# Row-wise infinity norm of an 8192 x 8192 matrix: smaller loads, more buffers, two load queues, and a tail in shrinking pieces

## The chip, the cores and the metric

The kernel runs on one core of a Trainium2 chip. The metric is the device time of one execution in microseconds (us), as a median over executions. A profile measures a span that is 1.7 to 2.1 us shorter than the time of the same execution. Its one-page summary is called the page here. Every run that is quoted here was fast, with the full clock granted (1.0 in the records).

Some words for what follows. In the traces each load appears as packets on 16 DMA engines: one packet for each partition's contiguous run of bytes, so 128 packets for a load of 128 partitions, eight on each engine (4,096 for the 32 loads of the kernel before). After its packets each engine makes a 4-byte semaphore write, the signal that VectorE waits for (528 writes in that trace, 16 for each of its 33 transfers). A load has landed when all 16 writes are in. A queue holds what one engine has issued. The exposed end is the reduce work that is left after the last landing.

## The reference

```python
def reference(x):                     # x: 8192 x 8192 float32, normally distributed
    return np.linalg.norm(x, ord=np.inf, axis=1)
```

For each row this is the largest absolute value in the row. The input is 268.4 MB and the output 32 KiB, so the work is to read the input once.

## The kernel before

The 8192 rows lie on 128 partitions, 64 rows on each. One load brings two neighbouring rows to every partition: 64 KiB per partition, 8 MiB in all. One VectorE reduce follows per load. There are three such buffers, and all loads go out from the SyncE queue.

```python
    x_t = x.rearrange("(a p n b) c -> a n p (b c)", p=P, a=A, n=N, b=B)   # A=8, N=4, B=2
    sbuf = ctx.enter_context(tc.tile_pool(name="sbuf", bufs=BUFS))        # BUFS=3
    r_all = outp.tile([P, A, N, B], mybir.dt.float32)

    for a in range(A):
        for n in range(N):
            t = sbuf.tile([P, bc], x.dtype)                               # bc = 16384
            t_b = t.rearrange("p (b c) -> p b c", b=B, c=cols)
            # ... a branch that is never taken is cut ...
            nc.sync.dma_start(out=t[:], in_=x_t[a, n])
            nc.vector.reduce_max(
                out=r_all[:, a, n, :], in_=t_b[:],
                axis=mybir.AxisListType.X, apply_absolute_value=True,
            )

    nc.sync.dma_start(out=out_t[:], in_=r_all[:])
```

Of the kernel before, what the change touches and what calls it, by code (L numbers as in the profile page):

```python
# [1 line left out]
logging.getLogger("concourse").setLevel(logging.ERROR)  # L3

# [1 line left out]

# [4 lines left out]


@with_exitstack
def kernel(
    ctx: ExitStack,
    tc: tile.TileContext,
    x: bass.AP,
    out: bass.AP,
    A: int = 8,
    B: int = 2,  # L20
    K: int = 4,
    BUFS: int = 3,
):
    nc = tc.nc
    P = nc.NUM_PARTITIONS

    rows, cols = x.shape
    assert rows % P == 0
    n_tiles = rows // P

    assert n_tiles % (A * B) == 0
    N = n_tiles // (A * B)
    x_t = x.rearrange("(a p n b) c -> a n p (b c)", p=P, a=A, n=N, b=B)
    out_t = out.rearrange("(a p n b) -> p a n b", p=P, a=A, n=N, b=B)

    bc = cols * B
    c_k = bc // K

    sbuf = ctx.enter_context(tc.tile_pool(name="sbuf", bufs=BUFS))
    outp = ctx.enter_context(tc.tile_pool(name="outp", bufs=1))  # L40

    r_part = outp.tile([P, N, K], mybir.dt.float32)
    r_all = outp.tile([P, A, N, B], mybir.dt.float32)

    for a in range(A):
        split = False
        for n in range(N):
            t = sbuf.tile([P, bc], x.dtype)
            t_b = t.rearrange("p (b c) -> p b c", b=B, c=cols)
            src = x_t[a, n]  # L50
            if split:
                for k in range(K):
                    nc.sync.dma_start(
                        out=t[:, k * c_k : (k + 1) * c_k],
                        in_=src[:, k * c_k : (k + 1) * c_k],
                    )
                    nc.vector.reduce_max(
                        out=r_part[:, n, k : k + 1],
                        in_=t[:, k * c_k : (k + 1) * c_k],
                        axis=mybir.AxisListType.X,  # L60
                        apply_absolute_value=True,
                    )
                nc.vector.reduce_max(
                    out=r_all[:, a, n, :],
                    in_=t_b[:],
                    axis=mybir.AxisListType.X,
                    apply_absolute_value=True,
                )
            else:
                nc.sync.dma_start(out=t[:], in_=src)  # L70
                nc.vector.reduce_max(  # L71
                    out=r_all[:, a, n, :],
                    in_=t_b[:],
                    axis=mybir.AxisListType.X,
                    apply_absolute_value=True,
                )

    nc.sync.dma_start(out=out_t[:], in_=r_all[:])


# [1 line left out]
_INS = ['x']  # L82
_OUTS = [((8192,), 'float32')]


# [23 lines left out]
```

## Time and profile before

| what | before | where it is read |
|---|---|---|
| time | 644.97 us | timed runs |
| span of the profiled run | 643.6 us | page |
| VectorE busy | 551.0 us | page, engines |
| first load packet starts | 1.76 us | packet records |
| last load packet ends / last load landed | 622.92 / 623.36 us | packet and semaphore records |
| reduce after that landing | 17.24 us | timeline |
| end of the last reduce to the end of the span | 2.98 us | timeline, page |

The page cuts the span into 40 slices. A digit is the busy share of a slice in tenths, and the last line is what the DMA engines moved in each slice, in GB/s:

```profile
DVE  0588898888998888998888988888988888988888
DMA  9999999999999999999999999999999999999960
GB/s 391 456 399 448 444 403 456 391 456 444 403 456 444 403 456 440 407 456 436 411 456 432 415 456 424 424 456 407 440 456 399 448 452 399 452 444 403 456 261 2
```

The DMA engines are at 9 until the end, while VectorE (DVE) is at 8 in most slices. The GB/s swing between slices because a packet of 64 KiB is booked where it lies: a slice is 16.1 us, in which six packets on each engine make 391 GB/s and seven make 456. The packets themselves are steadier. There are 4,096 packets of 65,536 bytes with a median of 2,420 ns, and their durations sum to 621.2 us per DMA engine, the same as the distance from the first packet's start to the last one's end. Followed along one engine, nearly every packet starts 3 to 4 ns before the record of the one before it ends. An engine is hardly ever without a packet. The loads are the bound.

The group of the reduces (line, engine, operation, names, shapes, count; busy us, mean ns of one; idle time before them and what ended it), and the profile's end in order of time (start us, duration, engine, line, operation, and in brackets the idle time before it):

```profile
L71 DVE TENSOR_REDUCE r_all<-t 128x2 f32<-128x16384 f32 x32 | 551.0, 17220 | 89.6 <-DMA t<-in_x_dram 89.6
```

```profile
604.03 17.22 DVE L71 TENSOR_REDUCE r_all<-t 128x2 f32<-128x16384 f32 x1 [2.12 <-DMA t<-in_x_dram]
623.38 17.22 DVE L71 TENSOR_REDUCE r_all<-t 128x2 f32<-128x16384 f32 x1 [2.13 <-DMA t<-in_x_dram]
640.62 0.40 SPq L78 DMA_DIRECT2D out_dram<-r_all  x1
```

VectorE waits 2.1 us for every load, so it is off the critical path everywhere except after the last landing. There a whole reduce of 17.22 us runs with nothing beside it, and then the output is stored. This 17.22 us is what the change can shorten. It should not lengthen the 621 us of loads.

### The profile page before, as it was taken

The page shows a single profiled execution, that of the slowest core. Times are in us where ns is not written, and L with a number is a line of the kernel's source. Part 1 is how long each engine was busy: PE and PEld are TensorE (multiplying, and loading weights), DVE is VectorE, ACT ScalarE, POOL GpSimd, SP SyncE. Part 2 cuts the span into 40 slices and gives each one's busy share as a digit, 9 for nine tenths or more (in the row PEclk, how much of TensorE's full clock was granted, in tenths as well). Part 3 has the DMA queues.
Part 4 walks back from the last instruction along what each step waited for, and adds up shares of the span by engine and source line. Part 5 has one row for each costly group of instructions (what it writes and reads, how often), then busy time and mean ns, then how long its engine had stood idle before and what let it go on. Part 6 is the DMA issues. An engine that isn't in the chain of part 4 may idle for free.

```text
span 643.6 us, 139 instructions
## 1 busy us (share of the span) xinstructions
DVE 551.0 (86%) x32; POOL 0.2 (0%) x4
## 2 busy tenths in 40 slices
DVE  0588898888998888998888988888988888988888
POOL 0000000000000000000000000000000000000000
DMA  9999999999999999999999999999999999999960
GB/s 391 456 399 448 444 403 456 391 456 444 403 456 444 403 456 440 407 456 436 411 456 432 415 456 424 424 456 407 440 456 399 448 452 399 452 444 403 456 261 2
DMA packets 5648, 268.47 MB, mean 417 GB/s; under 512 B 1552, under 2 KB 1552, under 8 KB 1552
## 3 DMA queue, kind: packets, MB, share of 16 engines
q1 hardware_dynamic: 5648, 268.47, 96.6%
HBM read 268.44 MB, written 0.03 MB: 417 GB/s over the span
## 4 chain that ended last, share of the span: by engine, by line
DMA 70%; DVE 29%; issue 0%; SPq 0%
DMA t<-in_x_dram 70%; DVE r_all L71 29%; SPq L70 0%
## 5 line engine op out<-in xcount | busy, mean ns | idle before, releaser
L71 DVE TENSOR_REDUCE r_all<-t 128x2 f32<-128x16384 f32 x32 | 551.0, 17220 | 89.6 <-DMA t<-in_x_dram 89.6
L93 POOL MEMSET const-bfloat16-1.0<- 128x1 bf16 x1 | 0.1, 102 | 0.0
L93 POOL MEMSET const-uint8-127<- 128x1 uint8 x1 | 0.1, 102 | 0.0
L93 POOL MEMSET const-float32-0.0<- 128x1 f32 x1 | 0.1, 99 | 0.2 <-issue 0.2
L93 POOL MEMSET const-float32-1.0<- 128x1 f32 x1 | 0.1, 99 | 0.0
## 6 DMA issues: line engine op xcount, KB each, us to landing
t<-in_x_dram SPq DMA_DIRECT2D x32, 40.8
out_dram<-r_all SPq DMA_DIRECT2D x1, 32.0 KB, 2.2
```

The source lines that it names most:

```text
L71: nc.vector.reduce_max(out=r_all[:, a, n, :], in_=t_b[:], axis=mybir.AxisListType.X, apply_absolute_value=True,)
L93: nc = _bacc.Bacc("TRN2", target_bir_lowering=False, num_devices=1)
```

## The change

Its intent is to leave little to reduce after the last landing. Loads become one row per partition (32 KiB per partition, 4 MiB), and the last rows are loaded and reduced in ever smaller pieces. Six buffers replace three, with nearly the same SBUF. Loads go out from SyncE and ScalarE in turn. The first 48 rows of each partition keep their layout. The last 16 rows form a tail whose partitions are 512 KiB apart in memory.

```diff
+TAIL = (
+    [[8192]] * 8
+    + [[4096, 4096]] * 5
+    + [[2048] * 4] * 2
+    + [[2048, 2048, 2048, 1024, 512, 512]]
+)
...
-    BUFS: int = 3,
+    G: int = 8,
+    BUFS: int = 6,
...
+    x_b = x[:split].rearrange("(a p n) c -> a n p c", p=P, a=A, n=G)
+    x_t = x[split:].rearrange("(p t) c -> t p c", p=P)
...
+    def absmax(o, i):
+        nc.vector.reduce_max(out=o, in_=i, axis=X, apply_absolute_value=True)
+
+    queues = (nc.sync, nc.scalar)
+    n_loads = 0
+
+    def load(o, i):
+        nonlocal n_loads
+        queues[n_loads % 2].dma_start(out=o, in_=i)
+        n_loads += 1
...
+        for n in range(G):
+            t = sbuf.tile([P, cols + 16], F32, tag="t")
+            load(t[:, :cols], x_b[a, n])
+            absmax(r_bulk[:, a, n : n + 1], t[:, :cols])
+
+    for r in range(n_tail):
+        t = sbuf.tile([P, cols + 16], F32, tag="t")
+        at = 0
+        last = r == n_tail - 1
+        for k, w in enumerate(TAIL[r]):
+            load(t[:, at : at + w], x_t[r][:, at : at + w])
+            if last and k == k_last - 1:
+                absmax(r_tail[:, : n_tail - 1], part[:])      # combines the pieces
+                nc.gpsimd.dma_start(out=out_b, in_=r_bulk[:])
+                nc.scalar.dma_start(out=out_t[:, : n_tail - 1], in_=r_tail[:, : n_tail - 1])
+                absmax(r_fin[:], t[:, at : cols + k_last - 1])  # last piece and the row's partial results
+            elif last:
+                absmax(t[:, cols + k : cols + k + 1], t[:, at : at + w])
+            else:
+                absmax(part[:, r, k : k + 1], t[:, at : at + w])
+            at += w
+    nc.sync.dma_start(out=out_t[:, n_tail - 1 :], in_=r_fin[:])
```

(Cuts are marked with dots. The lines removed are the loop shown above.)

More of the change, by code (lines that the diff above doesn't have):

```diff
@@ L10 @@
 from concourse._compat import with_exitstack
+F32 = mybir.dt.float32
+X = mybir.AxisListType.X
+TAIL = (
[4 more added lines that the diff above has]
+)
 @with_exitstack
@@ L18 @@
     out: bass.AP,
-    A: int = 8,
-    B: int = 2,
-    K: int = 4,
-    BUFS: int = 3,
+    G: int = 8,
+    BUFS: int = 6,
 ):
@@ L27 @@
     rows, cols = x.shape
-    assert rows % P == 0
-    n_tiles = rows // P
-    assert n_tiles % (A * B) == 0
-    N = n_tiles // (A * B)
-    x_t = x.rearrange("(a p n b) c -> a n p (b c)", p=P, a=A, n=N, b=B)
-    out_t = out.rearrange("(a p n b) -> p a n b", p=P, a=A, n=N, b=B)
-    bc = cols * B
-    c_k = bc // K
+    n_tail = len(TAIL)
+    n_bulk_rows = rows // P - n_tail
+    assert n_bulk_rows % G == 0
+    A = n_bulk_rows // G
+    split = n_bulk_rows * P
+    x_b = x[:split].rearrange("(a p n) c -> a n p c", p=P, a=A, n=G)
@@ L39 @@
+    out_b = out[:split].rearrange("(a p n) -> p a n", p=P, a=A, n=G)
+    x_t = x[split:].rearrange("(p t) c -> t p c", p=P)
+    out_t = out[split:].rearrange("(p t) -> p t", p=P)
     sbuf = ctx.enter_context(tc.tile_pool(name="sbuf", bufs=BUFS))
     outp = ctx.enter_context(tc.tile_pool(name="outp", bufs=1))
-    r_part = outp.tile([P, N, K], mybir.dt.float32)
-    r_all = outp.tile([P, A, N, B], mybir.dt.float32)
-    for a in range(A):
-        split = False
-        for n in range(N):
-            t = sbuf.tile([P, bc], x.dtype)
-            t_b = t.rearrange("p (b c) -> p b c", b=B, c=cols)
-            src = x_t[a, n]
-            if split:
-                for k in range(K):
-                    nc.sync.dma_start(
-                        out=t[:, k * c_k : (k + 1) * c_k],
-                        in_=src[:, k * c_k : (k + 1) * c_k],
-                    )
-                    nc.vector.reduce_max(
-                        out=r_part[:, n, k : k + 1],
-                        in_=t[:, k * c_k : (k + 1) * c_k],
-                        axis=mybir.AxisListType.X,
-                        apply_absolute_value=True,
-                    )
-                nc.vector.reduce_max(
-                    out=r_all[:, a, n, :],
-                    in_=t_b[:],
-                    axis=mybir.AxisListType.X,
-                    apply_absolute_value=True,
-                )
-            else:
-                nc.sync.dma_start(out=t[:], in_=src)
-                nc.vector.reduce_max(
-                    out=r_all[:, a, n, :],
-                    in_=t_b[:],
-                    axis=mybir.AxisListType.X,
-                    apply_absolute_value=True,
-                )
@@ L78 @@
-    nc.sync.dma_start(out=out_t[:], in_=r_all[:])
+    k_last = len(TAIL[-1])
+    r_bulk = outp.tile([P, A, G], F32)
+    r_tail = outp.tile([P, n_tail], F32)
+    r_fin = outp.tile([P, 1], F32)
+    k_max = max(len(r) for r in TAIL[:-1])
+    part = outp.tile([P, n_tail - 1, k_max], F32)
+    nc.vector.memset(part[:], 0.0)
+    def absmax(o, i):
[6 more added lines that the diff above has]
+        n_loads += 1
@@ new lines @@
+    for a in range(A):
+        for n in range(G):
[11 more added lines that the diff above has]
+                nc.gpsimd.dma_start(out=out_b, in_=r_bulk[:])
+                nc.scalar.dma_start(
+                    out=out_t[:, : n_tail - 1], in_=r_tail[:, : n_tail - 1]
+                )
+                absmax(r_fin[:], t[:, at : cols + k_last - 1])
+            elif last:
+                absmax(t[:, cols + k : cols + k + 1], t[:, at : at + w])
+            else:
+                absmax(part[:, r, k : k + 1], t[:, at : at + w])
+            at += w
```

## The prediction

> **What bounds it now.** The loads. The slice view has the DMA engines at 9 in every slice up to the last load, and the queue table gives the one load queue 96.6% of the span at 417 GB/s. The packet records show 4,096 packets of 64 KiB, median 2.42 us each; their durations sum to 621.2 us per engine, and the first starts 621.2 us before the last ends. So no engine ever starves: 16 x 65,536 B / 2.42 us = 433 GB/s. [...] VectorE is not the bound: 17.22 us per 8 MiB tile against about 19.35 us between landings (2.1 us idle before each, timeline view).
>
> Outside the stream: 1.8 us before the first packet, 0.4 us from last packet to landing (623.4), then an exposed reduce of 17.22 us, then 3.0 us for the output.
>
> **What the change does.**
> 1. Bytes, SBUF use and pitch of the bulk rows stay: no gain in the stream.
> 2. Packets halve to 32 KiB and shrink further at the end: some 640 data packets per engine instead of 256. If each costs 5 to 10 ns extra[...], that is an estimated +2 to +4 us. The tail's rows are 512 KiB apart instead of 256 KiB; I expect no loss there, without evidence.
> 3. VectorE: [...]some 48 more instructions: off the path, except at the end.
> 4. The exposed end. Ideally the last 512 columns (some 0.7 us) remain, a gain of 16.5 us. But the two queues spoil this. [...] If so, loads 2k and 2k+1 share the engines and land about together, every 19.4 us. VectorE then has two rows (17.4 us) of backlog at each pair's landing, as with the 8 MiB tile before. It gains on the loads only 9.7 - 8.7 = 1 us per row. Over the eight rows in pieces it recovers about 7 us of about 16. So some 9 us of reduce stay exposed: a gain of about 8 us, not 16.5.
> 5. The output: bulk results leave early from GpSimd; the last store has 128 small packets instead of 1,024: about -0.5 us.
>
> **Sum.** 645 - 8 + 2.5 - 0.5, rounded down for a chance that nothing pairs up: **638 us**, range 629.5 to 642. Faster by over 2%: 0.18; within 2%: 0.79; slower: 0.03.
>
> **What would show it.** Right: packet records with 32 KiB at 1.21 to 1.22 us; loads landing in twos, 1 to 2 us apart, then about 18 us nothing; the reduces of a pair back to back, an idle gap before the first only; the last reduce 7 to 10 us after the last landing, with no idle before the reduces of the final rows.
>
> **What would make it wrong.** The queues not sharing evenly, so that landings are staggered by 9.7 us: then 629 to 632. A larger cost per packet, or a slower tail from its 512 KiB pitch: the 16 engines' rate would fall below 430 GB/s in the last 155 us, up to 645.

(In point 2: 5 to 10 ns per packet is to be read as an assumption, and the +2 to +4 us as that times 384 more packets on each engine. The 8.7 us per row in point 4 is a little more than half of 17.22 us, 8.61 us, as each row then pays the fixed cost of a reduce. In point 4: the premise that the DMA engines take turns between two queues by packets, which rested on no trace. "If so" refers to it. The -0.5 us of point 5 is the author's estimate, without a measured number. 645 - 8 + 2.5 - 0.5 comes to 639 us, rounded down to 638.)

## The result, and the profile after

The changed kernel takes 638.88 us (638.73 to 638.96, 4 runs) against 644.97 us. The ratio is 0.9906, with a 95% interval of 0.9892 to 0.9920. That is faster by 0.9%, so within 2%. Ratios here are the mean time of one kernel's fast runs over that of the other's fast runs of the same rounds, so they are not quite the ratios of the medians that are quoted.

| what | before | after | difference |
|---|---|---|---|
| span of the profiled run | 643.6 | 637.2 | -6.4 |
| last load landed | 623.36 | 626.66 | +3.3 |
| reduces after that landing | 17.24 | 8.10 | -9.1 |
| end of the last reduce to the end of the span | 2.98 | 2.43 | -0.55 |

The three terms add up to the difference of the spans.

The slices, and the groups by shape:

```profile
DVE  0588998888988889988889888899888898899998
DMA  9999999999999999999999999999999999999992
GB/s 381 432 432 434 428 428 438 436 432 428 434 432 428 428 438 436 432 428 434 432 428 434 432 436 432 428 434 430 430 434 427 439 432 430 419 432 431 418 421 99
```

```profile
L61 DVE TENSOR_REDUCE r_bulk<-t 128x1 f32<-128x8192 f32 x48 | 414.7, 8681 | 71.2 <-DMA t<-in_x_dram 71.2
L61 DVE TENSOR_REDUCE part<-t 128x1 f32<-128x8192 f32 x8 | 69.1, 8681 | 9.0 <-DMA t<-in_x_dram 9.0
L61 DVE TENSOR_REDUCE part<-t 128x1 f32<-128x4096 f32 x10 | 43.3, 4409 | 0.0
L61 DVE TENSOR_REDUCE part<-t 128x1 f32<-128x2048 f32 x8 | 17.6, 2275 | 0.0
L61 DVE TENSOR_REDUCE t<-t 128x1 f32<-128x2048 f32 x3 | 6.7, 2275 | 0.0
```

The groups give the fixed cost of a reduce: 4,409 - 2,275 = 2,134 ns for 2048 columns, so about 140 ns of the 2,275 ns do not depend on the columns. They also show that VectorE never waits for a piece of 4096 columns or less: the idle time before them is 0.0. It is behind all through the pieces, so the last small piece finds a backlog. The timeline of the start and of the end shows why (columns as above; "x2" means two instructions back to back):

```profile
22.93 17.28 DVE L61 TENSOR_REDUCE r_bulk<-t 128x1 f32<-128x8192 f32 x2 [22.00 <-DMA t<-in_x_dram]
42.35 17.28 DVE L61 TENSOR_REDUCE r_bulk<-t 128x1 f32<-128x8192 f32 x2 [2.14 <-DMA t<-in_x_dram]
```

```profile
528.22 17.28 DVE L61 TENSOR_REDUCE part<-t 128x1 f32<-128x8192 f32 x2 [2.11 <-DMA t<-in_x_dram]
...
547.65 78.08 DVE L61 TENSOR_REDUCE part<-t 128x1 f32<-128x8192 f32 x20 [2.15 <-DMA t<-in_x_dram]
625.65 8.38 DVE L61 TENSOR_REDUCE t<-t 128x1 f32<-128x2048 f32 x5
633.95 0.20 DVE L61 TENSOR_REDUCE r_tail<-part 128x15 f32<-128x60 f32 x1
634.07 0.69 DVE L61 TENSOR_REDUCE r_fin<-t 128x1 f32<-128x517 f32 x1
634.19 0.35 ACTq L87 DMA_DIRECT2D out_dram<-r_tail  x1
634.79 0.35 SPq L96 DMA_DIRECT2D out_dram<-r_fin  x1
```

Two rows are reduced together, after one wait, every 19.4 us, as the two-row tile was before. From 547.65 us on VectorE does not stop until 634.76 us: 27 reduces, 87.1 us. The last load landed at 626.66 us, so 8.1 us remain after it.

The semaphore records of the trace give the landings directly:

```
landed, us:  22.91 23.07 | 42.33 42.49 | 61.72 61.90 | ... | 528.19 528.39 | 547.63 547.82 | ...
```

The rows land in twos, at most 0.2 us apart. The packet records show how. On each DMA engine one 32 KiB packet of the SyncE queue is followed by one of the ScalarE queue, and so on, with starts 1.21 us apart. The two rows share the engines and finish together.

The packet records also show what a packet costs (medians, ns):

```
bytes            2048   4096   8192   16384   32768   65536 (before)
one packet, ns     84    160    312     613    1215    2420
```

From 32 KiB to 64 KiB the time grows by 1,205 ns. Twice 1,215 less 2,420 is 10 ns that a packet costs beyond its bytes. The records overlap by 3 to 4 ns, so the landings are the safer measure: two rows take 19.42 us instead of 19.35 us, and 0.07 us over eight more packets (and one more semaphore write) is about 9 ns each. 32,768 bytes in 1,205 ns are 27.2 GB/s per engine, or 435 GB/s for 16. The change has 640 load packets per engine instead of 256, and the durations sum to 624.9 us instead of 621.2 us.

### The profile page after: what moved, and what is told of

It reads as the page before. It is cut to its first block, busy times and chain, and to the rows that moved or that the text cites. A ratio compares the mean times of both kernels' runs of the same rounds, so it can differ in the third digit from the quotient of the medians.

```text
span 637.2 us, 285 instructions
## 1 busy us (share of the span) xinstructions
DVE 553.7 (87%) x82; POOL 1.1 (0%) x5
## 4 chain that ended last, share of the span: by engine, by line
DMA 73%; DVE 25%; issue 1%; DVEq 0%
DMA t<-in_x_dram 73%; DVE part L61 13%; DVE r_bulk L61 11%; DVE t L61 1%; DVE r_fin L61 0%; DVE r_tail L61 0%; DVEq L61 0%
## 5 line engine op out<-in xcount | busy, mean ns | idle before, releaser
L61 DVE TENSOR_REDUCE r_bulk<-t 128x1 f32<-128x8192 f32 x48 | 414.7, 8681 | 71.2 <-DMA t<-in_x_dram 71.2
L61 DVE TENSOR_REDUCE part<-t 128x1 f32<-128x4096 f32 (+2 forms) x26 | 129.9, 5067 | 9.0 <-DMA t<-in_x_dram 9.0
L61 DVE TENSOR_REDUCE t<-t 128x1 f32<-128x2048 f32 (+2 forms) x5 | 8.4, 1741 | 0.0
```

Source lines behind the costliest of these rows:

```text
L61: nc.vector.reduce_max(out=o, in_=i, axis=X, apply_absolute_value=True)
```

## The experiments

The theory is that two queues take turns, row pairs land together, and VectorE therefore enters the pieces 17 us behind. It gains only 9.7 - 8.7 = 1 us per row on the loads, so eight rows of pieces cannot work this off. The packets explain the later landing. The rivals are these. A: VectorE is simply too slow for many small pieces, whatever the queues do. B: two queues help the stream. C: a second queue costs something by itself. D: the later landing comes from the second queue, from the distance between the tail's rows or from the store of the bulk results.

| run | edit to the changed kernel | median us | ratio to before, 95% | last landing | reduces after it |
|---|---|---|---|---|---|
| the change | - | 638.88 | 0.9906 (0.9892 to 0.9920) | 626.66 | 8.10 |
| e1 | one queue | 632.68 | 0.9811 (0.9796 to 0.9825) | 626.21 | 2.21 |
| e2 | whole rows, two queues | 647.50 | 1.0040 (1.0025 to 1.0055) | 625.47 | 17.19 |
| e3 | whole rows, one queue | 637.84 | 0.9890 (0.9873 to 0.9906) | 625.80 | 8.71 |
| e4 | first row in two column halves | 640.12 | 0.9926 (0.9911 to 0.9941) | 626.60 | 9.17 |
| e5 | tiny load of 64 partitions first | 636.72 | 0.9875 (0.9860 to 0.9889) | 626.64 | 5.98 |
| e5b | tiny load of 16 partitions first | 636.29 | 0.9869 (0.9853 to 0.9886) | 626.07 | 5.91 |
| e5c | tiny load of 32 partitions first | 635.20 | 0.9849 (0.9833 to 0.9866) | 626.96 | 4.73 |
| e5d | tiny load of 48 partitions first | 633.88 | 0.9831 (0.9816 to 0.9845) | 626.07 | 3.47 |
| e6 | one queue, first 48 rows in two-row loads | 630.05 | 0.9770 (0.9753 to 0.9786) | 623.49 | 2.24 |
| e8 | e3 with 8 KiB packets | 651.90 | 1.0110 (1.0094 to 1.0125) | 638.63 | 8.81 |

The ten runs e1 to e8 gave correct results. Against the kernel before, e6 is the only one that is clearly faster by more than 2%; the interval of e1 (0.9796 to 0.9825) lies across that line. The comparisons among the runs below are of medians, and the runs of one kernel lie within 1.1 us of one another. The landings and the reduces after them come from the profiled run of each.

### e1: one queue

```diff
-    queues = (nc.sync, nc.scalar)
+    queues = (nc.sync, nc.sync)
```

> The changed kernel with every load on the SyncE queue. Pairing theory (two queues share each DMA engine packet by packet, so two rows land together and VectorE is always up to 17 us behind): loads now land singly, 9.7 us apart for whole rows, the exposed end falls from 8.1 us to 1.5 to 2.5 us, time 632.5 to 633.5. Rival A (the exposed end is just VectorE too slow for small pieces, whatever the queue): exposed end stays near 8 us, time within 1 us of 638.9. Rival B (two queues help the stream, by hiding a packet's fixed cost): with one queue the 32 KiB packets grow beyond 1.215 us and the last landing moves later than 626.7 us. I expect the packets unchanged, last landing at 626 to 627.

It took 632.68 us, with the last landing at 626.21 us and 2.21 us of reduces after it. The timeline's start and end:

```profile
22.55 8.69 DVE L61 TENSOR_REDUCE r_bulk<-t 128x1 f32<-128x8192 f32 x1 [1.00 <-DMA t<-in_x_dram]
32.27 8.69 DVE L61 TENSOR_REDUCE r_bulk<-t 128x1 f32<-128x8192 f32 x1 [1.03 <-DMA t<-in_x_dram]
...
```

```profile
591.43 4.42 DVE L61 TENSOR_REDUCE part<-t 128x1 f32<-128x4096 f32 x1 [0.48 <-DMA t<-in_x_dram]
596.33 22.17 DVE L61 TENSOR_REDUCE part<-t 128x1 f32<-128x4096 f32 x9 [0.48 <-DMA t<-in_x_dram]
618.53 0.21 DVE L61 TENSOR_REDUCE r_tail<-part 128x15 f32<-128x60 f32 x1
618.70 2.29 DVE L61 TENSOR_REDUCE t<-t 128x1 f32<-128x2048 f32 x1
...
621.19 2.29 DVE L61 TENSOR_REDUCE t<-t 128x1 f32<-128x2048 f32 x1 [0.21 <-DMA t<-in_x_dram]
623.69 4.00 DVE L61 TENSOR_REDUCE t<-t 128x1 f32<-128x2048 f32 x3 [0.21 <-DMA t<-in_x_dram]
627.73 0.69 DVE L61 TENSOR_REDUCE r_fin<-t 128x1 f32<-128x517 f32 x1
```

Rows now come singly, 9.7 us apart, and VectorE waits for pieces right to the end, so it is not behind. Rival A falls: the same pieces on the same VectorE leave 2.2 us instead of 8.1 us. Rival B falls too: the 32 KiB packets have a median of 1,213 ns against 1,215 ns with two queues, and the last landing is no later. The second queue, as the change uses it, costs about 6.2 us (638.88 - 632.68), more than a third of the 16.5 us that the prediction named as the ideal gain.

### e2 and e3: whole rows, with two queues and with one

```diff
-TAIL = (
-    [[8192]] * 8
-    + [[4096, 4096]] * 5
-    + [[2048] * 4] * 2
-    + [[2048, 2048, 2048, 1024, 512, 512]]
-)
+TAIL = [[8192]] * 16
```

e3 has the edit of e1 as well.

> The changed kernel without the shrinking tail: all 64 rows are whole, two queues. Pairing theory: the last two rows land within 0.2 us of one another and 17.3 us of reduce follow, as in the kernel before; fewer packets (512 per engine) bring the last landing to about 625.3; the output tail is 2.4 us; time 646 to 647, slower than before by about 0.3%. Rival A (VectorE only, no pairing): 8.7 us exposed, time about 638.

> Whole rows, one queue. Pairing theory: only the last row's 8.7 us are exposed, last landing about 625.3, time 637.5 to 638.5: as good as the whole change without its shrinking tail and without its second queue. Rival A: the same as the run with two queues and whole rows, within 1 us.

e2 took 647.50 us, and its last two rows landed at 625.29 and 625.47 us with 17.2 us of reduces after that. It was predicted at 646 to 647 us; the half microsecond over was not followed. e3 took 637.84 us with 8.7 us exposed. With e1 and the change these make a two-by-two table:

| median us | two queues | one queue |
|---|---|---|
| whole rows | 647.50 | 637.84 |
| shrinking pieces | 638.88 | 632.68 |

With two queues and whole rows, halving the load gains nothing over the kernel before: the pair of rows is the old two-row tile again, with more packets. One queue without any shrinking tail (637.84 us) does as well as the whole change.

These two runs also settle a part of rival D. Their tail rows are whole and 512 KiB apart, and they were read at 432.0 and 432.2 GB/s in e2 (520 to 560 and 560 to 600 us, from the packet records), against 432.1 GB/s for rows 256 KiB apart. (From 480 to 520 us, where the bulk results are stored, e2 shows 430.9 and e3 422.5 GB/s. The profiled run of e3 was the slowest of its four by 0.75 us, so its dip was not in every execution.)

### e4: half a row, to put the queues out of step

```diff
+            if a == 0 and n == 0:
+                load(t[:, :half], x_b[0, 0][:, :half])        # half = 4096 columns
+                absmax(first[:, 0:1], t[:, :half])
+                continue
...
+        if r == 8:                                            # after the whole rows
+            t = sbuf.tile([P, cols + 16], F32, tag="t")
+            nc.sync.dma_start(out=t[:, half:cols], in_=x_b[0, 0][:, half:])
+            absmax(first[:, 1:2], t[:, half:cols])
+            absmax(r_bulk[:, 0, 0:1], first[:])
```

> The changed kernel with both queues kept, but the first row's load cut in half, its second half sent after the whole rows: so the SyncE queue runs half a row ahead of the ScalarE queue. Pairing theory (it is the equal phase, not the second queue as such): whole rows land alternately, about 9.7 us apart, VectorE's backlog before the pieces is about 8.7 us instead of 17.3, exposed end 1.5 to 3 us, time 632.5 to 634. Rival C (a second queue costs by itself): exposed end and time stay near 8 us and 638.9.

This missed: 640.12 us, 9.2 us exposed. (The 1.2 us above the change was not followed.) But it was no test of rival C, because the queues stayed in step. The half row landed at 17.88 us and the whole row beside it at 18.05 us. A half row over 128 partitions is as many packets as a whole one, eight per engine, of half the size. In the packet records the 16 KiB packets of one queue alternate one for one with the 32 KiB packets of the other, and the semaphore write of the half row waits for its own turn after the last of them. One engine, followed from packet to packet:

```
start us   13.47   14.08   15.29   15.90   17.11
bytes      16384   32768   16384   32768       4
queue      SyncE  ScalarE  SyncE  ScalarE  SyncE
```

So the engines took turns here by packets and not by bytes. To put the queues out of step one needs a different number of packets, which costs little if they are tiny (8 to 11 ns each in the runs below).

### e5, e5b, e5c, e5d: a tiny load to put the queues out of step by packets

```diff
+    tiny = outp.tile([64, 16], F32)                     # 64; then 16, 32, 48
...
+    nc.scalar.dma_start(out=tiny[:], in_=x[:64, :16])   # result unused
```

> The changed kernel with both queues and one tiny load (64 partitions x 64 B, unused) ahead of the ScalarE queue's first load. The run with half a row at the start kept its pairs (landings 17.88 and 18.05 us), which a turn by packets explains: half a row is as many packets as a row, only shorter. The tiny load has 4 packets per DMA engine, so ScalarE's queue should be 4 of 8 packets behind for the whole run at almost no cost in time. Pairing theory, by packets: whole rows land alternately about 9.7 us apart, exposed end 1.5 to 3 us, time 632.5 to 634. Rival C (a second queue costs by itself, or engines fall back into step): pairs within 1 us of one another, exposed end near 8 us, time near 638.9.

It took 636.72 us. The rows landed 2.4 us apart (31.22 and 33.63 us), not 9.7. In the packet records three packets of the SyncE queue go out before the tiny load's first one (at 5.9 us), then each of its four packets and its semaphore write takes a turn against a 32 KiB packet. ScalarE's first row starts when SyncE's first row is complete, so its queue was 7 packets behind where 4 were wanted. The pairs had only slid by nearly a whole row.

> The same with a tiny load of 16 partitions instead of 64: one packet per DMA engine. The run before put ScalarE's queue 7 of 8 packets behind, not 4: three packets of the SyncE queue went out before the tiny load's first, then its four packets and its semaphore write each took a turn. Its pairs were 2.4 us apart instead of 0.2 and its exposed end was 6.0 us. With one packet the lag should be 4 packets: whole rows landing alternately 8 to 11 us apart, exposed end 1.5 to 3 us, time 632.3 to 634, that is the time of the one-queue run with both queues in use. If a second queue costs by itself: still near 8 us and 638.9.

It took 636.29 us, also short of the expectation. This time the tiny packet went out right after the first SyncE packet (at 3.5 us), so the queues were only 2 packets out of step, and the rows landed 4.9 us apart. The reduces after the last landing were no shorter than in e5, although the spacing was twice as large. The unbroken stretch of VectorE at the end explains it. It starts with the first landing of the last pair, at 544.87 us, and again takes 87.11 us, the same as with the change. If the mean of the two landings stays, a spacing s moves the first one by s/2 only. With this the last two runs were predicted.

> The tiny load has 32 partitions, two packets per DMA engine. With 16 partitions ScalarE's queue ran only 2 packets behind (landings 4.9 us apart, time 636.3), with 64 it ran 7 behind, which is 1 to 2 short of the next row (2.4 us, 636.7). VectorE runs without a stop from the first landing of the last pair of whole rows, and then needs 87.1 us in every one of these runs; a spacing s moves that first landing earlier by half of s only. So: time = 638.9 less s/2, within 0.7 us, while s is below a reduce's 8.7 us. For 3 packets behind, s is 7.3 us and the time 635.2; for 5 behind the same from the other side. If a second queue costs by itself, the time does not follow s and stays at 636 or more.

> The tiny load has 48 partitions, three packets per DMA engine. For 4 packets behind, s is 9.7 us, more than a reduce: rows land as with one queue, and the time should be that of the one-queue run, 632.7 (632.2 to 633.5). For 6 behind (if the tiny load's first packet is late, as with 64 partitions), s is 4.9 us from the other side and the time 636 to 636.5.

| run | rows land apart | unbroken stretch from | to | time | 638.9 less half the spacing |
|---|---|---|---|---|---|
| the change | 0.2 | 547.65 | 634.76 | 638.88 | 638.8 |
| e5 | 2.4 | 536.92 (one row earlier) | 632.62 | 636.72 | 637.7 |
| e5b | 4.9 | 544.87 | 631.98 | 636.29 | 636.5 |
| e5c | 7.3 | 544.58 | 631.69 | 635.20 | 635.3 |
| e5d | 9.7 | 542.43 | 629.54 | 633.88 | 634.1 |

The starts of the stretch themselves moved by 2.8, 3.1 and 5.2 us in e5b, e5c and e5d, where half the spacing is 2.4, 3.7 and 4.9 us, so the rule holds to about half a microsecond. e5c met its number. (Its profiled execution, at 635.97 us, was the slowest of its four.) e5d came out 0.4 us above its range, and 1.2 us above one queue. Its whole rows land and are reduced one by one, as the timeline shows:

```profile
532.71 8.69 DVE L62 TENSOR_REDUCE part<-t 128x1 f32<-128x8192 f32 x1 [1.03 <-DMA t<-in_x_dram]
...
542.43 78.08 DVE L62 TENSOR_REDUCE part<-t 128x1 f32<-128x8192 f32 x20 [1.04 <-DMA t<-in_x_dram]
620.43 8.38 DVE L62 TENSOR_REDUCE t<-t 128x1 f32<-128x2048 f32 x5
```

The last whole row landed at 549.73 us, only 7.3 us after the one before it. When the SyncE queue reached its half-row pieces, its packets were half as long (16 KiB and 32 KiB packets have medians of 613 and 1,215 ns in the change), so ScalarE's packets of a whole row came round faster. VectorE was then still busy until 551.1 us, and that lag stays until the end. So rival C falls for the larger part: with both queues in use and an unused tiny load on top, 5.0 of the 6.2 us come back. That much is the cost of the equal phase of the queues, not of the second queue. The remaining 1.2 us fits this last transition: the reduce of the last whole row starts 1.4 us after its landing (551.1 less 549.73). This is argued from the timeline and not shown by a run of its own. e5 lies 1 us better than the line. In it the last pair is made up differently (the stretch starts one row earlier, with 28 reduces), and this was not taken further.

### e8: eight-KiB packets

Here each whole row of e3 is loaded by four loads of 2048 columns, and reduced once.

```diff
-            load(t[:, :cols], x_b[a, n])
+            for k in range(4):
+                load(t[:, k * 2048 : (k + 1) * 2048], x_b[a, n][:, k * 2048 : (k + 1) * 2048])
...                                                  # the same for the tail's rows, and the edits of e3
```

> One queue, whole-row reduces, but each row is loaded in four pieces of 2048 columns: 2,048 packets of 8 KiB per engine instead of 512 of 32 KiB. Packet theory: 1,536 more packets at 10 to 12 ns, so the last landing moves from 625.8 to 641 to 645 us and the time from 637.8 to 653 to 658. Rival (the later last landing of the change, 626.7 against 623.4 before, came from the second queue, the distance of 512 KiB between the tail's rows or the stores of the bulk results): within 2 us of 637.8.

It took 651.90 us, with the last landing at 638.63 us. The last landing moved by 12.8 us and the median time by 14.1 us: over 1,536 more packets that is 8.4 to 9.2 ns each, with the semaphore writes of the extra loads (one for every eight packets, as in the change). The durations sum to 640.3 us per engine instead of 624.0 us, 10.6 ns for each extra packet, but these records overlap by 3 to 4 ns, so the landings are taken here. The expectation had used 10 to 12 ns, and its time lay 1 to 6 us too high. The direction and the scale are those of the packet theory. One queue and the same rows in more packets make the stream longer: 384 more packets at 8.4 to 9.2 ns are 3.2 to 3.5 us, which is the +3.3 us of the change.

One part of rival D is left. The pair of rows that was being loaded in the change while the bulk results were stored (packets of that store from 492.4 to 496.0 us) landed 19.86 us after the pair before it, instead of 19.42 us. The row at that place was late by 0.5 to 0.6 us in e1 and e5d, and by 0.1 us in e6. On the other side, the profile of the kernel before has about 0.9 us of slower loads in its first 140 us. So the packets are the larger part of the +3.3 us, but the agreement is no closer than a microsecond, and no run here takes the store away.

### e6: what the experiments point to

One queue, the tail of the change unchanged, but the first 48 rows of each partition in two-row loads with three buffers, as before. These packets are 64 KiB again.

```diff
-    queues = (nc.sync, nc.scalar)
+    queues = (nc.sync, nc.sync)
-    BUFS: int = 6,
+    N: int = 4,
+    B: int = 2,
+    BUFS: int = 3,
...
-    x_b = x[:split].rearrange("(a p n) c -> a n p c", p=P, a=A, n=G)
+    x_b = x[:split].rearrange("(a p n b) c -> a n p (b c)", p=P, a=A, n=N, b=B)
...
-            t = sbuf.tile([P, cols + 16], F32, tag="t")
-            load(t[:, :cols], x_b[a, n])
-            absmax(r_bulk[:, a, n : n + 1], t[:, :cols])
+            t = sbuf.tile([P, B * cols + 16], F32, tag="t")
+            load(t[:, : B * cols], x_b[a, n])
+            absmax(r_bulk[:, a, n * B : (n + 1) * B],
+                   t[:, : B * cols].rearrange("p (b c) -> p b c", b=B))
...                                                  # two tail rows share a tile
```

> One queue, the first 48 rows per partition in loads of two rows (64 KiB packets, three buffers, as the kernel before), the change's tail of 16 rows unchanged. Packet theory (each packet costs some 10 ns beyond its bytes): 192 packets per engine fewer than with one queue and one-row loads, so the last landing is 1.5 to 2.5 us earlier than its 626.2. The backlog of VectorE at the end of the two-row loads is 17 us instead of 8.7, which the eight whole rows of the tail must work off first; if 16 rows are enough, the exposed end stays at 2 to 3 us and the time is 630 to 631.5, the fastest. If packets cost nothing: last landing unchanged, time 632.5 to 633.5.

It took 630.05 us (ratio 0.977, 0.9753 to 0.9786) and is the fastest of all, clear of both kernels. The last landing is 2.7 us earlier than in e1. That is a little over the expected 1.5 to 2.5 us, and 0.8 us more than 192 packets at 10 ns. Here too the profile with more packets shows 0.6 us lost at the store of the bulk results, and the one of e6 0.1 us. The end:

```profile
593.98 21.96 DVE L63 TENSOR_REDUCE part<-t 128x1 f32<-128x4096 f32 x9 [0.40 <-DMA t<-in_x_dram]
...
621.00 4.01 DVE L63 TENSOR_REDUCE t<-t 128x1 f32<-128x2048 f32 x3 [0.23 <-DMA t<-in_x_dram]
625.04 0.69 DVE L63 TENSOR_REDUCE r_fin<-t 128x1 f32<-128x517 f32 x1
```

VectorE enters the tail 17 us behind here too, but it gains 1 us per row over the tail's eight whole rows, which now land singly. It waits for a load again (0.37 us) before the eighth of them, at 545.24 us, and among the pieces at 589.16 and 593.98 us.

## Why the prediction was right

The prediction was 638 us with a range of 629.5 to 642, and the kernel measured 638.88 us. Point by point:

1. "What bounds it now." Right. The stream set the pace up to the tail in every run, and the fastest run is a stream up to 623.49 us with 2.2 us of reduces and 2.6 us of stores after it. In the change itself VectorE sets the last 87.1 us.
2. "Packets", an estimated +2 to +4 us. The last landing moved by 3.3 us and the durations by 3.7 us. 32 KiB packets were predicted at 1.21 to 1.22 us and took 1.215 us. e8 supports the cause, with the store of the bulk results as a part that was not foreseen (about 0.4 us). No loss from the 512 KiB distance was expected "without evidence", and none was found (432 GB/s in e2).
3. "The exposed end", a gain of about 8 us instead of 16.5 us. It was 9.1 us, from 17.24 to 8.10 us. The cause, two queues taking turns and rows landing in twos, is seen in the packets and the landings. e1 shows that it costs the 6 us, and e5 to e5d show that 5.0 of them are the equal phase.
4. "About -0.5 us" for the output: -0.55 us.
5. Two details were off. "Loads landing in twos, 1 to 2 us apart" was 0.2 us. On each engine the semaphore write of the first row takes its own turn, after the last packet of the other row, so both semaphores go out together (one engine of the change: both writes at 41.00 us). And "it recovers about 7 us of about 16" was nearer 9 of 17.

The sum of the terms, +3.3 - 9.1 - 0.55 = -6.4 us, is the difference of the spans. The times differ by 6.1 us; the 0.3 us between is not explained. The profiled span of the kernel before, 643.6 us, is also 0.8 us longer than the spans of its later timed runs (642.6 to 643.4, mostly 642.8), with slow packets in its first 140 us. So the split between the terms is good to about a microsecond.

The mechanism was right, but the closeness of the number, 0.9 us, is partly luck. The stream grew by 0.8 us more than the 2.5 us in the sum, and the exposed end gave 1.1 us more than the 8 us in it, and these two errors nearly cancel. The last step, rounding 639 down to 638 for a chance that nothing pairs up, went the wrong way: everything paired up.

## What to carry to other kernels

The two queues here, with equal streams, did not deliver alternately. They delivered in pairs, and a consumer that is a little faster than the stream (8.7 us against 9.7 us per row) then stayed one unit behind. Where the last landing's work is what is exposed, put the loads on one queue (632.68 us instead of 638.88 us here), or give the queues different numbers of packets ahead (633.88 us at best). The second is fragile: a tiny load of 4, 1, 2 or 3 packets per engine put the queues 7, 2, 3 or 4 packets apart, so the landings must be read from a trace. A shrinking tail works off a backlog only at the difference between the load's and the consumer's pace (here 1 us per 9.7 us row), so count how many rows that takes, and keep packets large before it (one more packet cost about 9 ns here, 8.4 to 9.2 ns in e8).
